# Sums of weight blocks made in DRAM by accumulating transfers, for twelve quads of a hybrid decoder trunk

## The chip, the cores and the metric

The kernel runs on one core of a Trainium2 chip. The metric is device time in microseconds of the whole program, the median of several runs. Engines are named as the profile names them: PE (TensorE), DVE (VectorE), ACT (ScalarE), POOL (GpSimd) and SP (SyncE). SP and POOL issue the DMA transfers here; the bytes are moved by 16 DMA engines that both queues share.

## The reference

Two layers on 512 tokens of width 1024, all float32. Layer 0 mixes with an mLSTM, layer 1 with a gated short convolution, and each is followed by a squared-ReLU MLP of width 4096:

```python
for i in range(DEPTH):
    h = rms_norm(x, g[0])
    h = mlstm_mixer(h, ...) if i % 2 == 0 else short_conv_mixer(h, ...)
    x = x + rms_norm(h, g[1])
    h = sqrelu_mlp(rms_norm(x, g[2]), w_mlp_up[i], w_mlp_down[i])
    x = x + rms_norm(h, g[3])
```

The products that matter here are `x @ w_up` (1024 x 4096, in both MLPs) and the convolution's input projection `x @ w_in` (1024 x 3072). In the mLSTM, each head's output is divided by its root mean square (`h * rsqrt(mean(h * h) + EPS)`) before the gate and the out projection.

## The kernel before

**Precision.** Every product is made of three fp32r products. A loaded weight block is split in a high half (ACT's cast, line 80) and a low half (DVE's subtraction, line 81), and `mm3` (lines 112 to 117) multiplies high by high, high by low and low by high.

**Quads.** The up projections and the convolution's input projection are computed by quads: a quad takes a 1024 x 512 piece of the weight as four blocks a, b, c, d of 512 x 256 (a and b the upper row half, c and d the lower) and forms the 2 x 2 block product with seven block products instead of eight. Four of the seven weight factors are sums of blocks: with the names of the new class `Sums` below f5 = a + b, f6 = f5 + d, f7 = b + d, f3 = f6 + c; the others are a, c and d themselves. Each block is loaded by SP into a "raw" tile of 512 KB (seven such buffers), DVE makes the sums in place (lines 899, 905, 920, 931 in `run`; lines 852 to 858 in `sums`, for a stage's first quad), and each factor is split as above.

**Stages.** There are three stages of quads: the MLP of layer 0 (eight quads), the convolution (six), and the MLP of layer 1 (eight). The first three quads of a stage (`AHEAD`) are prepared in `enter` while the stage before ends: their factors a and c are loaded and split, and their first two products run early. Later `run_first` and `run(True)` finish them.

**The mLSTM part**, in the first 187 us, holds no quads. It normalises x tile by tile (`pre_norm`; the power of the norm is a one-column operation of POOL, line 173), projects the first half of v, then the gates and q, k, then the second half of v with the chunk scores (`scores_and_core`), then the output gates, eight column pieces. `core` computes one chunk for two heads; its norm takes a power on POOL (line 714), between DVE's lines 713 and 715. The scaled result is transposed, gated and multiplied by the out projection.

**What sets the order.** The program is written as data flow; a scheduler places each engine's instructions by its own estimate of when they can start, and then each engine runs its list strictly in order. A transfer waits on its issuing engine, SP or POOL, until what it reads has landed and its buffer is free, and whatever stands behind it on that engine waits too. SP's transfers use eight semaphores in turn, and so do POOL's, so that at most eight of a queue are under way.

Of the kernel before, what the change touches and what calls it, by code (L numbers as in the profile page):

```python
# [8 lines left out]
F32 = mybir.dt.float32  # L9
# [3 lines left out]
ALU = mybir.AluOpType  # L13
# [26 lines left out]
def tile_hybrid_trunk(  # L40
# [239 lines left out]
    def last_product(wm, r0, hT, g, tail, accs=None, ends=False, ahead=None):  # L280

        flush()
        ws = {}
        parts = [halves() for _ in range(NT)]
        if ends:
            parts[NT - 1] = halves()[:1] + halves(4)[2:]
        ygs = [[] for _ in range(NT)]
        mss = [None] * NT

        def ks(o, t, cs, k0, k1):  # L290
            hf, c0 = divmod(cs.start, 512)
            n = cs.stop - cs.start
            for k in range(k0, k1):
                w = ws[hf][k // 2]
                mm3(
                    o[:, 0:n],
                    rows_of(hT, k, t),
                    (w[:, 0, k % 2, c0 : c0 + n], w[:, 1, k % 2, c0 : c0 + n]),
                    k == 0,
                    k == KO - 1,  # L300
                )

        def done(o, t, cs):
            n = cs.stop - cs.start
            step(BLOCK * n / 512)
            i = len(ygs[t])
            if i == 0:
                mss[t] = small(len(parts[t]))
            yg = half_kb(n=n) if accs is None else accs[t][:, cs]
            ygs[t].append((cs, yg))  # L310
            last = i == len(parts[t]) - 1
            o = o[:, 0:n]
            if accs is None:
                part_ms(o, mss[t], i)
                nc.vector.tensor_tensor(out=yg, in0=o, in1=g[:, cs], op=ALU.mult)  # L315
            else:
                y = accs[t][:, cs]
                nc.vector.tensor_tensor(out=y, in0=y, in1=o, op=ALU.add)  # L318
                part_ms(y, mss[t], i)
                eng = nc.vector if ends and t == NT - 1 else nc.gpsimd  # L320
                eng.tensor_tensor(out=yg, in0=y, in1=g[:, cs], op=ALU.mult)
            if last:
                tail(t, ygs[t], mss[t])

        for hf in range(2):
            ws[hf] = [
                piece(
                    wm[r0 + 2 * i * P : r0 + 2 * (i + 1) * P, halves()[hf]].rearrange(
                        "(k p) m -> p k m", p=P
                    ),  # L330
                    2,
                )
                for i in range(4)
            ]
            os = [pd() for _ in range(2)]
            first = KO - 2 if hf == 0 else 0
            for t in range(2):
                ks(os[t], t, parts[t][hf], 0, first)
            for t in range(2):
                ks(os[t], t, parts[t][hf], first, KO)  # L340
                done(os[t], t, parts[t][hf])
        for t in range(2, NT):
            if ahead is not None:
                ahead()
            for cs in parts[t]:
                o = pd()
                ks(o, t, cs, 0, KO)
                done(o, t, cs)


    wi = w_in_mlstm[0]
# [392 lines left out]
    def gated(j, sg):  # L744
# [7 lines left out]
        )  # L752
        put_pair(hT, j, pr)

    def scores_and_core(t):
        scores(t)
        if t > 0:
            core(t - 1, 0)

    v_half(1, [piece(v_src(1, i), 2) for i in range(4)], lambda t: None, scores_and_core)  # L760
    for j in range(KO):
        w = cols_piece(wi, 2 * QK + D + j * P)
        o = pu()
        proj_T(o, w, xT, 0, NT)
        take_o(j, o, BLOCK if j < KO - 1 else 0)
        if j <= NT:
            core((j - 1) % NT, 0 if j == 0 else 1)

# [37 lines left out]
    class Quad:  # L806

        def __init__(self, wm, c0, c1, xT, take, claim=lambda: None):  # L810
            self.wm, self.cols, self.xT, self.take = wm, (c0, c1), xT, take
            self.claim = claim

        def block(self, kh, nh):
            c = self.cols[nh]
# [30 lines left out]
            self.v = self.values()  # L846
            nc.scalar.copy(self.v, by_tile(self.x))

        def sums(self):
            tt = nc.vector.tensor_tensor  # L850
            a, b = self.block(0, 0), self.block(0, 1)
            tt(out=a, in0=a, in1=b, op=ALU.add)
            d = self.block(1, 1)
            t2 = raw_tile([4, 256])
            tt(out=t2, in0=a, in1=d, op=ALU.add)
            tt(out=b, in0=b, in1=d, op=ALU.add)
            c = self.block(1, 0)
            tt(out=c, in0=c, in1=t2, op=ALU.add)
            self.ts = c, a, t2, b, d

        def run_first(self):

            tt = nc.vector.tensor_tensor
            f = self.xT.f
            self.claim()
            o, z, y = pd(), pd(), self.y
            f4, f5, f6, f7, f3 = (self.factor(t) for t in self.ts)
            prod(o, f4, f["a22"], True)
            prod(z, f5, f["p1"], True)
            s5 = self.values()  # L870
            nc.scalar.copy(s5, by_tile(z))
# [12 lines left out]
            tt(out=s3, in0=by_tile(o), in1=s3, op=ALU.add)  # L884
            self.take(0, 1, s3, None)

        def run(self, begun):


            tt = nc.vector.tensor_tensor  # L890
            f = self.xT.f
            bank = pd if begun else pu
            self.claim()
            a, b = self.block(0, 0), self.block(0, 1)
            if not begun:
                self.f1 = self.factor(a)
                self.begin(pu)
            y = self.y
            tt(out=a, in0=a, in1=b, op=ALU.add)  # L899
            f5 = self.factor(a)  # L900
            z = bank()
            if not begun:
                prod(z, f5, f["p1"], True)
            d = self.block(1, 1)
            tt(out=a, in0=a, in1=d, op=ALU.add)  # L905
            f6 = self.factor(a)
            prod(y, f6, f["n2"], False)
            s5, s2 = self.values(), self.values()
            if begun:
                nc.scalar.copy(s2, by_tile(y))  # L910
                prod(z, f5, f["p1"], True)
            nc.scalar.copy(s5, by_tile(z))
            if not begun:
                nc.scalar.copy(s2, by_tile(y))
            c = self.block(1, 0)
            if not begun:
                self.f2 = self.factor(c)
                self.second()
                self.take(0, 0, self.values(), by_tile(self.x))
            tt(out=b, in0=b, in1=d, op=ALU.add)  # L920
            prod(y, self.factor(b), f["r3"], False)
            o = bank()
            nc.scalar.mul(by_tile(o), by_tile(y), -1.0)
            prod(z, self.factor(d), f["p4"], False)
            tt(out=s5, in0=by_tile(y), in1=s5, op=ALU.add)
            self.take(1, 1, s5, None)
            tt(out=s2, in0=by_tile(z), in1=s2, op=ALU.add)
            self.take(1, 0, s2, None)
            if begun:
                self.take(0, 0, self.v, None)  # L930
            tt(out=a, in0=a, in1=c, op=ALU.add)  # L931
            prod(o, self.factor(a), f["a22"], False)
            self.take(0, 1, self.values(), by_tile(o))

    def enter(quads):


        for qd in quads:
            qd.prepare()
        yield  # L940
        for qd in quads:
            qd.prepare_more()
        quads[0].sums()
        yield
        flush(2)
        for qd, bank in zip(quads, (pd, pd, pu)):
            qd.begin(bank)
        for qd in quads:
            qd.second()
            qd.put_by()  # L950
        flush()
# [4 lines left out]
    def mlp(i, xT, gain_of, tail_of, ends=False, ahead=None):  # L956
# [4 lines left out]
        def quad(g):  # L961
# [10 lines left out]
                    hs[j] = pair()  # L972
                split(hs[j][:, 0, half], hs[j][:, 1, half], c)

            return Quad(w_up[i], g * 512, g * 512 + 256, xT, take)

        ys = []

# [30 lines left out]
        quads[0].run_first()  # L1009
        quads[1].run(True)  # L1010
        for g in range(NG - 2):
            down(g)
            quads[g + 2].run(g + 2 < AHEAD)
            if g == NG - 4:
# [4 lines left out]
    def conv(xT, gain_of, tail_of, ahead):  # L1019
# [5 lines left out]
        def gated(p):  # L1025
# [33 lines left out]
                            op1=ALU.add,  # L1059
                        )  # L1060

            return Quad(wm, D + p * 256, 2 * D + p * 256, xT, take, claim)

        def out_gate(b):
            def take(nh, half, v, o):
# [4 lines left out]
                    yT[j] = pair()  # L1070
                split(yT[j][:, 0, half], yT[j][:, 1, half], v)

            return Quad(wm, b * 512, b * 512 + 256, xT, take)

        quads = [gated(0), gated(1), gated(2), out_gate(0), gated(3), out_gate(1)]
        first = quads[:AHEAD]
# [51 lines left out]
```

## Time and profile before

| | |
|---|---|
| median of 3 runs | 1106.7 us (1105.1 to 1108.88) |
| the profiled execution | 1111.46 us, its span 1109.7 us |
| granted TensorE clock, mean | 0.994 |
| moved by DMA | 133.73 MB, 121 GB/s over the span |
| read from HBM, written | 124.31 MB, 8.39 MB |

A span runs from the first to the last instruction. Times within the profile are microseconds from the span's start. In a timeline row the first two numbers are start and length, and the square bracket gives the engine's idle time before the instruction and what ended it. In a row of groups stand count, busy time, mean nanoseconds of one, and idle time ahead of it. Matmuls overlap, so that PE's busy time is not its work at full rate.

### The profile page before, as it was taken

The numbers are of one execution on the slowest core, as the hardware profiler recorded it, in microseconds if no ns is written. First come the engines' busy times: TensorE is split into PE (matmuls) and PEld (weight loads), VectorE is DVE, ScalarE is ACT, GpSimd is POOL, SyncE is SP. The second block draws the span as 40 slices with busy tenths as digits, with TensorE's granted clock in tenths as the row PEclk, the third lists the DMA queues.
The fourth block names the chain that finished last, engine by engine and source line by source line (L and its number), as shares of the span: only waits on it lengthen the run. The fifth ranks groups of instructions, "written<-read, shape, count | busy, mean of one in ns | idle before, by whom it ended". The sixth has DMA issues, their size and how long they took to land. (4 is left out here: it accounts for less than half of the span.)

```text
span 1109.7 us, 16027 instructions
## 1 busy us (share of the span) xinstructions
PE 1080.6 (97%) x6531; PEld 951.8 (86%) x6531; DVE 758.5 (68%) x1008; ACT 503.8 (45%) x780; POOL 70.3 (6%) x114
## 2 busy tenths in 40 slices
PE   7999999999999999999999999899999999999997
PEld 5878887789899899899879999778989989989986
DVE  5561567489776775758579998848967667575843
ACT  6441445365554244335346545636554434424521
POOL 1100010110000000000231000011000000000011
PEclk9999999999999999999999999989999999999999
DMA  8420264136344133163424362623533413415201
GB/s 266 134 76 1 76 228 138 71 102 198 117 135 134 46 126 125 47 208 110 144 89 153 95 209 96 200 105 104 182 117 128 135 56 114 133 44 203 96 19 57
DMA packets 104783, 133.73 MB, mean 121 GB/s; under 512 B 5221, under 2 KB 76165, under 8 KB 104710
## 3 DMA queue, kind: packets, MB, share of 16 engines
q1 hardware_dynamic: 100246, 116.46, 33.3%
q0 software_dynamic: 4464, 16.25, 4.0%
q8 instruction: 51, 0.84, 0.3%
q14 instruction: 22, 0.18, 0.1%
HBM read 124.31 MB, written 8.39 MB: 120 GB/s over the span
## 5 line engine op out<-in xcount | busy, mean ns | idle before, releaser
L81 DVE TENSOR_TENSOR u<-raw,u 128x1024 fp32r<-128x1024 f32 (+1 forms) x270 | 320.5, 1200 | 123.5 <-ACT u L80 123.1
L80 ACT CAST u<-raw 128x1024 fp32r<-128x1024 f32 (+1 forms) x270 | 272.3, 1028 | 216.2 <-PE pd L117 159.3
L115 PE MATMUL pu<-u 128*128 128x256 f32 (+1 forms) x1112 | 337.2, 303 | 3.5 <-ACT u L80 3.4
L116 PE MATMUL pu<-u 128*128 128x256 f32 (+1 forms) x1112 | 335.6, 302 | 0.8 <-DVE u L81 0.8
L117 PE MATMUL pu<-u 128*128 128x256 f32 (+1 forms) x1112 | 334.7, 301 | 0.8 <-DVE u L81 0.8
L115 PE MATMUL pd<-u,hb 128*128 128x512 f32 (+1 forms) x648 | 256.1, 395 | 5.5 <-DVE t L315 4.4
L116 PE MATMUL pd<-u,hb 128*128 128x512 f32 (+1 forms) x648 | 255.2, 394 | 0.0
L117 PE MATMUL pd<-u,hb 128*128 128x512 f32 (+1 forms) x648 | 255.1, 394 | 0.0
L115 PEld LDWEIGHTS pu<-u 128*128 128x128 f32 x1112 | 210.6, 189 | 13.7 <-ACT u L80 4.8
L116 PEld LDWEIGHTS pu<-u 128*128 128x128 f32 x1112 | 210.4, 189 | 10.1 <-DVE u L81 1.6
L117 PEld LDWEIGHTS pu<-u 128*128 128x128 f32 x1112 | 210.5, 189 | 9.6 <-DVE u L81 1.3
L115 PEld LDWEIGHTS pd<-u,hb 128*128 128x128 f32 x648 | 122.4, 189 | 35.2 <-DVE t L315 5.3
L117 PEld LDWEIGHTS pd<-u,hb 128*128 128x128 f32 x648 | 122.3, 189 | 28.2
L116 PEld LDWEIGHTS pd<-u,hb 128*128 128x128 f32 x648 | 122.5, 189 | 27.9 <-DVE u L81 0.6
L115 PE MATMUL pd<-u 128*128 128x256 f32 x312 | 88.3, 283 | 4.1 <-ACT pu L840 2.4
L116 PE MATMUL pd<-u 128*128 128x256 f32 x312 | 87.5, 281 | 0.0
L117 PE MATMUL pd<-u 128*128 128x256 f32 x312 | 87.3, 281 | 0.0
L1004 DVE TENSOR_TENSOR u<-u,pd 128x512 f32<-128x512 f32 x80 | 54.6, 683 | 36.8 <-PE pd L117 36.5
L181 ACT ACTIVATE junk<-u 128x512 bf16<-128x512 f32 (+1 forms) x49 | 30.5, 622 | 74.1 <-DVE u L318 53.3
L80 ACT CAST hb<-t 128x512 fp32r<-128x512 f32 x80 | 48.9, 619 | 32.5 <-DVE t L968 26.7
L115 PEld LDWEIGHTS pd<-u 128*128 128x128 f32 x312 | 58.8, 188 | 5.2 <-ACT pu L840 2.8
L116 PEld LDWEIGHTS pd<-u 128*128 128x128 f32 x312 | 58.8, 188 | 0.0
(173 smaller groups left out, 851.7 us busy)
## 6 DMA issues: line engine op xcount, KB each, us to landing
raw<-in_w_mlp_up_dram SPq DMA_DIRECT2D x76, 512.0 KB, 4.5
raw<-in_w_mlp_down_dram SPq DMA_DIRECT2D x64, 512.0 KB, 4.2
raw<-in_w_in_conv_dram SPq DMA_DIRECT2D x30, 512.0 KB, 4.8
raw<-in_w_in_mlstm_dram SPq DMA_DIRECT2D x24, 512.0 KB, 4.7
xd<-u POOLq DMA_DIRECT2D x12, 512.0 KB, 3.0
u<-xd POOLq DMA_DIRECT2D x12, 512.0 KB, 5.8
raw<-in_w_out_mlstm_dram SPq DMA_DIRECT2D x8, 512.0 KB, 4.1
raw<-in_w_out_conv_dram SPq DMA_DIRECT2D x8, 512.0 KB, 4.6
```

The costliest lines, as they stand in the source:

```text
L80: hi = nc.scalar.copy(dst_hi, src)
L81: lo = nc.vector.tensor_tensor(out=dst_lo, in0=src, in1=dst_hi.bitcast(F32), op=ALU.subtract)
L115: nc.tensor.matmul(o, lh, rh, start=first, stop=False, skip_group_check=True)
L116: nc.tensor.matmul(o, lh, rl, start=False, stop=False, skip_group_check=True)
L117: nc.tensor.matmul(o, ll, rh, start=False, stop=last, skip_group_check=True)
L181: nc.scalar.activation(junk(n), src, AF.Square, scale=float(D) ** -0.5, accum_out=ms[:, i : i + 1])
L1004: nc.vector.tensor_tensor(out=yh, in0=yh, in1=o, op=ALU.add)
```

## The change

For twelve quads (the three prepared ones of each MLP and all six of the convolution) the four sums are made in DRAM. `Sums` holds four DRAM tiles of 512 KB. Its stage 0 copies a, d, b and c into them on SP's queue, DRAM to DRAM; stages 1 to 3 add the rest by accumulating transfers on POOL's queue: b to f5 and d to f7, then f5 to f6, then f6 to f3. The quad then loads its four sums (`summed`), and a, c and d themselves where it needs them, seven loads in place of four blocks; the adds on DVE are gone for these quads. The sums of the first MLP are written in the loop of the second v half (stages 0 to 2) and of the output gates (stage 3); the nine others in the first MLP's `down` loop.

```diff
+    class Sums:
+        def __init__(self, wm, c0, c1):
+            def src(kh, c):
+                return wm[kh * 512 : (kh + 1) * 512, c : c + 256].rearrange("(p q) m -> q p m", q=P)
+            self.a, self.b, self.c, self.d = src(0, c0), src(0, c1), src(1, c0), src(1, c1)
+            self.f = [
+                dram.tile([P, 4, 256], F32, name=f"f{n}_{len(made)}") for n in (5, 6, 7, 3)
+            ]
+        def stage(self, i):
+            f5, f6, f7, f3 = self.f
+            if i == 0:
+                for f, blk in zip(self.f, (self.a, self.d, self.b, self.c)):
+                    nc.sync.dma_start(f, blk)
+                return
+            for f, blk in (((f5, self.b), (f7, self.d)), ((f6, f5),), ((f3, f6),))[i - 1]:
+                nc.gpsimd.dma_start(f, blk, accum_op=ALU.add, max_dma_last_dim=D)
...
     def scores_and_core(t):
+        if t != 2:
+            all_of(early, min(t, 2))
         scores(t)
...
         take_o(j, o, BLOCK if j < KO - 1 else 0)
+        if j == 3:
+            all_of(early, 3)
...
+        def summed(self, i):
+            raw = raw_tile([4, 256])
+            nc.sync.dma_start(raw, self.pre.f[i])
+            return self.factor(raw)
...
-            f4, f5, f6, f7, f3 = (self.factor(t) for t in self.ts)
+            f4, f5, f6, f7 = (self.summed(i) for i in (3, 0, 1, 2))
+            f3 = self.factor(self.block(1, 1))
...
-            tt(out=a, in0=a, in1=b, op=ALU.add)
-            f5 = self.factor(a)
+            if not pre:
+                tt(out=a, in0=a, in1=b, op=ALU.add)
+            f5 = self.summed(0) if pre else self.factor(a)
...
-        quads[0].sums()
...
         for g in range(NG - 2):
+            if i == 0:
+                for k in range(3):
+                    if 0 <= g - k < 4:
+                        all_of(later[3 * k : 3 * k + 3], g - k)
             down(g)
```

The new lines shift the rest: the norm's power on POOL is line 743 after the change (714 before), DVE's step behind it line 744 (715), the copies are line 367 and the accumulating transfers line 370.

On SP's queue before the change, in the mLSTM part: the q and k pieces and the second v half's four pieces (shape 128x2x512) are followed at once by the eight output-gate pieces (128x8x128) and the out projection.

```order
L98 DMA raw<-in_w_in_mlstm_dram 128x8x128 x8
L98 DMA raw<-in_w_in_mlstm_dram 128x2x512 x2
L724 DMA t_702<-in_w_conv_dram 24x128
L725 DMA t_702<-in_g_hnorm_dram 8x128
L98 DMA raw<-in_w_in_mlstm_dram 128x2x512 x2
L98 DMA raw<-in_w_in_mlstm_dram 128x8x128 x8
L98 DMA raw<-in_w_out_mlstm_dram 128x2x512 x3
```

After the change, the same place; `f_3` to `f_11` are the sums of the convolution's quads and of the second MLP's, four tiles to a number. Shown are the last of the four v pieces with what follows it, and then the end of that run of copies.

```order
L98 DMA raw<-in_w_in_mlstm_dram 128x2x512
L367 DMA f_2_720<-in_w_mlp_up_dram 512x1x256
L367 DMA f_3_721<-in_w_in_conv_dram 512x1x256
L367 DMA f_3_722<-in_w_in_conv_dram 512x1x256
L367 DMA f_3_723<-in_w_in_conv_dram 512x1x256
```

```order
L367 DMA f_11_753<-in_w_mlp_up_dram 512x1x256
L367 DMA f_11_754<-in_w_mlp_up_dram 512x1x256
L98 DMA raw<-in_w_in_mlstm_dram 128x8x128 x3
L367 DMA f_11_755<-in_w_mlp_up_dram 512x1x256
L367 DMA f_11_756<-in_w_mlp_up_dram 512x1x256
L98 DMA raw<-in_w_in_mlstm_dram 128x8x128 x5
```

Between the last v piece and the first three output-gate pieces now stand 35 copies, those of the convolution and of the second MLP among them; all 48 copies are ahead of the fourth output-gate piece.

On POOL before the change, in the same part: the memsets of the gate rows, the four selections of the decay matrix (line 610), the eight powers of the head norm (line 714), and then the first out-projection norm.

```order
L522 MEMSET u 4x512
L589 MEMSET sel 36x512
L523 MEMSET u 4x4
L610 AFFINE_SELECT hb<-hb 128x512 x4
L714 TENSOR_TENSOR small<-small,mhalf 128x2 x8
L173 TENSOR_TENSOR small<-small,mhalf 128x1
```

After the change, around the first two of the eight powers (now line 743):

```order
L370 DMA f_7_740<-f_7_738 512x256
L370 DMA f_9_747<-in_w_mlp_up_dram 512x1x256
L370 DMA f_8_744<-f_8_742 512x256
L743 TENSOR_TENSOR small<-small,mhalf 128x2
L370 DMA f_10_749<-in_w_mlp_up_dram 512x1x256
L370 DMA f_9_746<-f_9_745 512x256
L370 DMA f_10_751<-in_w_mlp_up_dram 512x1x256
L370 DMA f_10_750<-f_10_749 512x256
L370 DMA f_11_753<-in_w_mlp_up_dram 512x1x256
L370 DMA f_9_748<-f_9_746 512x256
L370 DMA f_10_752<-f_10_750 512x256
L743 TENSOR_TENSOR small<-small,mhalf 128x2
```

Of the 48 accumulating transfers, four stand among the four powers of the first norm, 34 between these and the first head-norm power, seven between the first and the second, three between the second and the third; the other powers follow without any between them. The list of DVE in this part reads as before.

More of the change, by code (lines that the diff above doesn't have):

```diff
@@ L348, in last_product, with sums_of @@
                 done(o, t, cs)
+    class Sums:
[14 more added lines that the diff above has]
+                nc.gpsimd.dma_start(f, blk, accum_op=ALU.add, max_dma_last_dim=D)
+    made = {}
+    def sums_of(key, wm, cols):
+        for c in cols:
+            made[key, c[0]] = Sums(wm, *c)
+        return [made[key, c[0]] for c in cols]
     wi = w_in_mlstm[0]
@@ L753, in gated, with up_cols, all_of @@
         put_pair(hT, j, pr)
+    def up_cols(gs):
+        return [(g * 512, g * 512 + 256) for g in gs]
+    early = sums_of(0, w_up[0], up_cols(range(AHEAD)))
+    later = sums_of(
+        "conv",
+        w_in_conv[0],
+        [(D + p * 256, 2 * D + p * 256) for p in range(3)]
+        + up_cols([0])
+        + [(D + 768, 2 * D + 768)]
+        + up_cols([1]),
+    ) + sums_of(1, w_up[1], up_cols(range(AHEAD)))
+    def all_of(sums, i):
+        for sm in sums:
+            sm.stage(i)
     def scores_and_core(t):
+        if t != 2:
+            all_of(early, min(t, 2))
         scores(t)
@@ L806, in tile_hybrid_trunk, with __init__ @@
     class Quad:
-        def __init__(self, wm, c0, c1, xT, take, claim=lambda: None):
+        def __init__(self, wm, c0, c1, xT, take, key, claim=lambda: None):
             self.wm, self.cols, self.xT, self.take = wm, (c0, c1), xT, take
             self.claim = claim
+            self.pre = made.get((key, c0))
         def block(self, kh, nh):
@@ L847, in put_by @@
             nc.scalar.copy(self.v, by_tile(self.x))
[L849 to L859, printed above, removed]
+        def summed(self, i):
+            raw = raw_tile([4, 256])
+            nc.sync.dma_start(raw, self.pre.f[i])
+            return self.factor(raw)
         def run_first(self):
@@ L892, in run @@
             bank = pd if begun else pu
+            pre = self.pre is not None
             self.claim()
-            a, b = self.block(0, 0), self.block(0, 1)
+            if not pre:
+                a, b = self.block(0, 0), self.block(0, 1)
             if not begun:
-                self.f1 = self.factor(a)
+                self.f1 = self.factor(self.block(0, 0) if pre else a)
                 self.begin(pu)
             y = self.y
-            tt(out=a, in0=a, in1=b, op=ALU.add)
-            f5 = self.factor(a)
+            if not pre:
+                tt(out=a, in0=a, in1=b, op=ALU.add)
+            f5 = self.summed(0) if pre else self.factor(a)
             z = bank()
@@ L903, in run @@
                 prod(z, f5, f["p1"], True)
-            d = self.block(1, 1)
-            tt(out=a, in0=a, in1=d, op=ALU.add)
-            f6 = self.factor(a)
+            if not pre:
+                d = self.block(1, 1)
+                tt(out=a, in0=a, in1=d, op=ALU.add)
+            f6 = self.summed(1) if pre else self.factor(a)
             prod(y, f6, f["n2"], False)
@@ L914, in run @@
                 nc.scalar.copy(s2, by_tile(y))
-            c = self.block(1, 0)
+            if not pre or not begun:
+                c = self.block(1, 0)
             if not begun:
@@ L919, in run @@
                 self.take(0, 0, self.values(), by_tile(self.x))
-            tt(out=b, in0=b, in1=d, op=ALU.add)
-            prod(y, self.factor(b), f["r3"], False)
+            if not pre:
+                tt(out=b, in0=b, in1=d, op=ALU.add)
+            prod(y, self.summed(2) if pre else self.factor(b), f["r3"], False)
             o = bank()
             nc.scalar.mul(by_tile(o), by_tile(y), -1.0)
-            prod(z, self.factor(d), f["p4"], False)
+            prod(z, self.factor(self.block(1, 1) if pre else d), f["p4"], False)
             tt(out=s5, in0=by_tile(y), in1=s5, op=ALU.add)
@@ L930, in run @@
                 self.take(0, 0, self.v, None)
-            tt(out=a, in0=a, in1=c, op=ALU.add)
-            prod(o, self.factor(a), f["a22"], False)
+            if not pre:
+                tt(out=a, in0=a, in1=c, op=ALU.add)
+            prod(o, self.summed(3) if pre else self.factor(a), f["a22"], False)
             self.take(0, 1, self.values(), by_tile(o))
@@ L973, in take @@
                 split(hs[j][:, 0, half], hs[j][:, 1, half], c)
-            return Quad(w_up[i], g * 512, g * 512 + 256, xT, take)
+            return Quad(w_up[i], g * 512, g * 512 + 256, xT, take, i)
         ys = []
@@ L1060, in take @@
                         )
-            return Quad(wm, D + p * 256, 2 * D + p * 256, xT, take, claim)
+            return Quad(wm, D + p * 256, 2 * D + p * 256, xT, take, "conv", claim)
         def out_gate(b):
@@ L1071, in take @@
                 split(yT[j][:, 0, half], yT[j][:, 1, half], v)
-            return Quad(wm, b * 512, b * 512 + 256, xT, take)
+            return Quad(wm, b * 512, b * 512 + 256, xT, take, "conv")
         quads = [gated(0), gated(1), gated(2), out_gate(0), gated(3), out_gate(1)]
```

## The prediction

> **What bounds the kernel now.** I read the page's first part, then the busy time by stages, then the timelines of GpSimd, VectorE and SyncE in the first 140 us, because the change puts nearly all its new transfers there.
>
> ```profile
> span 1109.7 us, 16027 instructions
> PE 1080.6 (97%) x6531; PEld 951.8 (86%) x6531; DVE 758.5 (68%) x1008; ACT 503.8 (45%) x780; POOL 70.3 (6%) x114
> ```
>
> TensorE is busy all but 29.1 us of the span, so a lighter VectorE can give back little, and only where TensorE waits for it. By stages (columns: stretch, its length, busy us of PE, PEld, DVE, ACT, POOL, granted clock, DMA share, GB/s):
>
> ```profile
> 0.00:28.00 28.00, 22.04 (x77) 14.37 (x78) 15.50 (x28) 17.48 (x34) 4.96 (x19) 1.00 0.88 263
> 8.00:14.00 6.00, 4.78 (x13) 3.10 (x12) 3.63 (x4) 4.56 (x8) 0.00 (x0) 1.00 1.03 395
> 28.00:56.00 28.00, 28.00 (x126) 22.78 (x125) 14.52 (x22) 13.33 (x17) 3.33 (x7) 1.00 0.46 133
> 56.00:84.00 28.00, 26.52 (x114) 20.39 (x113) 17.20 (x26) 10.81 (x26) 2.49 (x4) 1.00 0.28 76
> 84.00:112.00 28.00, 28.00 (x134) 22.74 (x133) 5.79 (x17) 3.44 (x9) 0.79 (x2) 1.00 0.00 1
> 224.00:308.00 84.00, 82.04 (x554) 74.54 (x553) 70.53 (x89) 49.50 (x79) 5.38 (x8) 1.00 0.45 144
> 560.00:588.00 28.00, 26.64 (x155) 22.87 (x154) 23.77 (x34) 16.71 (x34) 10.81 (x12) 1.00 0.26 87
> 588.00:672.00 84.00, 79.67 (x670) 78.88 (x668) 78.30 (x93) 48.03 (x67) 4.25 (x12) 1.00 0.47 153
> 672.00:728.00 56.00, 51.78 (x348) 48.09 (x347) 43.30 (x47) 28.62 (x38) 0.00 (x0) 0.91 0.53 170
> 756.00:812.00 56.00, 54.54 (x430) 52.54 (x428) 52.24 (x70) 31.35 (x50) 3.00 (x5) 1.00 0.49 156
> ```
>
> The last five rows hold the twelve quads: VectorE is 77 to 93% busy there and TensorE idles 2.0 + 1.4 + 4.3 + 4.2 + 1.5 = 13.4 us. That, and 5 us of lost clock in 672 to 728 (0.09 x 56), is all that fewer adds could return. The first rows are the mLSTM part, where the DMA is nearly idle from 56 to 112 us and TensorE full.
>
> In that part TensorE hangs on a short VectorE-GpSimd chain, the power of the head norm (line 714, on GpSimd). Timelines of GpSimd and VectorE:
>
> ```profile
> 110.38 0.72 POOL L714 TENSOR_TENSOR small<-small,mhalf 128x2 f32<-128x2 f32 x1 [26.32 <-DVE small L713]
> 120.68 0.70 POOL L714 TENSOR_TENSOR small<-small,mhalf 128x2 f32<-128x2 f32 x1 [9.58 <-DVE small L713]
> 132.83 0.69 POOL L714 TENSOR_TENSOR small<-small,mhalf 128x2 f32<-128x2 f32 x1 [11.44 <-DVE small L713]
> ```
> ```profile
> 111.14 0.16 DVE L715 TENSOR_TENSOR small<-small 128x2 f32<-128x2 f32 x1 [0.84 <-POOL small L714]
> 111.34 0.62 DVE L718 TENSOR_SCALAR u<-u,small 128x256 f32<-128x256 f32 x2
> 115.36 0.69 DVE L641 TENSOR_TENSOR raw<-pd,hb 128x512 f32<-128x512 f32 x1 [3.40 <-PE pd L638]
> ```
>
> VectorE takes its instructions in order: line 715 waits for the first power, and behind it stands line 641, which empties a PSUM bank that TensorE fills again at once. VectorE idles 3.40 us before line 641, so the first power may come up to 3.4 us late, at 113.8 us, before TensorE stops.
>
> **The change part by part.** *Adds removed.* Each of twelve quads loses four adds on 128x1024, as in these groups and in lines 852 to 858:
>
> ```profile
> L899 DVE TENSOR_TENSOR raw<-raw 128x1024 f32<-128x1024 f32 x19 | 23.1, 1217 | 0.3 <-DMA raw<-in_w_in_conv_dram 0.2
> L852 DVE TENSOR_TENSOR raw<-raw 128x1024 f32<-128x1024 f32 x3 | 3.7, 1217 | 0.0
> ```
>
> 48 x 1.217 = 58 us of VectorE work go. Of the 13.4 us and 5 us above I credit 7 us net, because TensorE's waits there also end at ScalarE's copies and at PSUM, and because new idle stretches will cost clock. The range of this term is 0 to 18.
>
> *Loads.* Nine quads load seven blocks where they loaded six, three load seven where they loaded four: 18 more transfers of 512 KB in stages where the DMA share is at most 0.53. Hidden; their buffers come free after one split instead of several adds.
>
> *Copies and accumulates.* 48 copies on SyncE's queue and 48 accumulating transfers on GpSimd's, 512 KB each. The order shows where they stand: all of them in the mLSTM part, those for the convolution and the second MLP too, since nothing in them depends on the stage in which they are written. On SyncE's queue 35 copies stand between the last value-weight load (issued at 55.17 us) and the first three output-gate loads. On GpSimd's, 34 accumulates stand between the last power of the first norm (line 173) and the first head-norm power, 7 more ahead of the second, 3 more ahead of the third. An accumulate waits for its copy and, two or three rows on, for the accumulate before it; the powers queue behind. That GpSimd holds everything behind a waiting transfer is seen already in the view of waits, where its loads of x wait for TensorE:
>
> ```profile
> POOL u L776 <- PE pu L117: 470.3, 5, 229.9
> ```
>
> The load on SyncE's queue behind which the copies now stand (timeline of SyncE), the queue's totals (packets, MB, share of 16 engines) and GpSimd's issue of a 128-row transfer (groups):
>
> ```profile
> 55.17 0.39 SPq L98 DMA_DIRECT2D raw<-in_w_in_mlstm_dram  x1
> ```
> ```profile
> q1 hardware_dynamic: 100246, 116.46, 33.3%
> ```
> ```profile
> L785 POOL DMA_DIRECT2D xd<-u x12 | 7.0, 584 | 24.1 <-DVE u L274 24.1
> ```
>
> The price of a transfer: SyncE's queue moved 116.46 MB in 33.3% of 1109.7 us, 315 GB/s while busy, so 1.66 us for 512 KB (0.524 MB). The fastest stretch, 8 to 14 us with the queue never empty, moved 395 GB/s: 1.33 us. With the queue kept full I take 1.5 for a copy. No row shows an accumulate. Below: one pass, like a copy, at 1.33. Above: three passes (source, destination, write) at 1.66, 5.0 us. I take two passes, 3.0 us, as both addends must be read.
>
> DMA work ahead of the first power, counted from 28 us: the loads of before, 0.46 x 28 + 0.28 x 28 = 20.7, less three output-gate loads that now queue behind (5.0), 15.7; what the first 28 us (12% of them free, 3.4 us) can't hold of the first quad's four copies and four accumulates, 6 + 12 - 3.4 = 14.6; 35 copies, up to the one that the last of these accumulates needs, 52.5; 34 accumulates, 102. Sum 185 us: the first power at 213 instead of 110.4, 99 us past 113.8. The second power: seven accumulates, each sharing with a copy or load, 7 x 4.5 = 31.5 against 10.3 before, +21. The third: 3 x 4.5 plus latency against 12.2, +4. Then GpSimd is free and the rest runs as before. GpSimd's own issuing (0.58 us for a transfer of 128 rows; these have 512, so up to 2.3) stays below 4.5 and is hidden.
>
> *The start.* Four copies (6 us) go ahead of the last two x loads, and four accumulates between GpSimd's powers of the first norm. Most of it falls on tiles whose turn on TensorE comes later, so I take 2 us; the bounds are 0 and 8.
>
> Sum: 99 + 21 + 4 + 2 - 7 = +119 us. The profiled execution took 1111.46 us for a span of 1109.7, 4.8 above the median of 1106.7; the terms are differences, so I add them to the median: 1226 us.
>
> The Trainium skill ("DMA: Bandwidth & Descriptors", Anatomy of one DMA) fits a GpSimd transfer as 2.0 us plus bytes over 436 GB/s, 1.2 us of streaming for 512 KB, an estimate that counts one pass; by 1.2 for copies and accumulates alike the sum would be about +21, 1128 us. This trace's best stretch (395 GB/s) stays below that rate, and no run here shows it for DRAM to DRAM.
>
> **The rivals.** *One pass* (0.2): an accumulate costs what a copy costs. Work ahead of the first power at 1.33: 15.7 + 7.2 + 46.6 + 45.2 = 115, power at 143, 29 late; second +8; with +2 and -7 that is +32, 1139 us. At 1.66 it is 1169. For it: 395 GB/s were reached. Against: two operands must come in. The Trainium skill's fit ("DMA: Bandwidth & Descriptors", Anatomy of one DMA) counts bytes once and so describes this rival.
>
> *Three passes or worse* (0.18): accumulates of 5.0 us, or descriptors that GpSimd writes as slowly. Copies at 1.66: 15.7 + 23.1 + 58.1 + 169 = 266, power at 294, 180 late; second +36, third +8; 1326 us. Nothing in the trace speaks for or against.
>
> *Hidden, and faster* (0.05): the idle DMA takes the sums for nothing and the twelve quads get their 58 us of VectorE back. The price is the -7 (0 to -18): 1100 us. It decides at 113.8 us: the 69 transfers would have to land in 86 us less the 15.7 of other loads, 1.0 us each or 515 GB/s, above any stretch of the trace. It needs the accumulates not to gate the power.
>
> *No effect* (0.02): sums hidden and TensorE's waits in the quads not VectorE's adds at all, 1107.
>
> **How the numbers follow.** Two passes has 0.55 (1200 to 1250 with copies from 1.33 to 1.66). Leaving out the outer tails of the two neighbours, the range is 1140 to 1325. All three DMA cases are slower: 0.93. This kernel's runs resolve about 0.3%, 3.3 us; within that 0.02, faster 0.05.
>
> **What would show it.** DMA share near 1 from about 30 us to past 200 us where it was 0.00 to 0.46. The first power (now line 743) near 213 us, released by a DMA or by GpSimd's own queue; VectorE's line 744 idle for about 100 us ahead of it, and TensorE with it. From the second half of the out projection on, the stages as long as before, the quads' a little shorter. Wrong, if the first power is issued before 120 us, if TensorE's loss lies after 300 us, or if the accumulates land in under 2 us each with the queue full.

## The result, and the profile after

The changed kernel takes 1224.1 us (median, 1221.7 to 1224.8) where the kernel before takes 1107.8: ratio 1.105, 95% interval 1.101 to 1.108. It is slower by 116 us; +119 was forecast. The profiled execution took 1224.8 us, with a span of 1223.1.

From the page of the changed kernel's profile: engines, granted clock and DMA share in 40 slices of 30.6 us, and the two queues (packets, MB, share of 16 engines).

```profile
PE 1090.4 (89%) x6531; PEld 959.8 (78%) x6531; DVE 708.9 (58%) x960; ACT 504.1 (41%) x780; POOL 121.7 (10%) x162
...
PEclk9899655689999999999999999999999999999999
DMA  9999999976227244223416256773373333135111
...
q1 hardware_dynamic: 116662, 151.07, 39.0%
q0 software_dynamic: 29808, 41.42, 16.5%
```

VectorE's 48 adds are gone and its busy time is 50 us lower, as meant. The DMA digits read 9 through the first eight slices, 245 us, where the page of before has a 2 in the third and a 0 in the fourth. POOL's queue went from 4.0 to 16.5% of the engines' time. The loss is early, as the busy time by stages shows (columns as in the prediction):

```profile
28.00:56.00 28.00, 22.06 (x86) 17.94 (x87) 9.24 (x15) 7.90 (x14) 6.18 (x13) 0.82 1.10 279
...
84.00:112.00 28.00, 28.00 (x124) 21.69 (x123) 2.60 (x5) 6.14 (x19) 5.87 (x6) 1.00 1.16 265
112.00:140.00 28.00, 5.82 (x27) 4.41 (x25) 0.72 (x2) 0.59 (x1) 9.09 (x10) 0.68 1.17 248
...
168.00:196.00 28.00, 0.00 (x0) 0.00 (x0) 0.00 (x0) 0.00 (x0) 8.93 (x8) 0.50 1.18 238
```

TensorE does nothing from 168 to 196 us while the DMA share is 1.18. What it hangs on are POOL's selections of the decay matrix (line 639) and powers of the head norm (line 743), shown first in POOL's timeline, then in VectorE's, then as seen by TensorE in the view of waits:

```profile
137.06 2.19 POOL L639 TENSOR_SCALAR_AFFINE_SELECT hb<-hb 128x512 f32<-128x512 f32 x2
...
203.87 1.03 POOL L370 DMA_DIRECT2D f<-f  x1 [8.73 <-DMA f<-f]
204.52 1.13 POOL L743 TENSOR_TENSOR small<-small,mhalf 128x2 f32<-128x2 f32 x1
236.27 1.13 POOL L743 TENSOR_TENSOR small<-small,mhalf 128x2 f32<-128x2 f32 x1
252.01 1.11 POOL L743 TENSOR_TENSOR small<-small,mhalf 128x2 f32<-128x2 f32 x1
...
299.82 0.69 POOL L743 TENSOR_TENSOR small<-small,mhalf 128x2 f32<-128x2 f32 x1 [9.55 <-DVE small L742]
```
```profile
139.28 0.69 DVE L670 TENSOR_TENSOR raw<-pd,hb 128x512 f32<-128x512 f32 x1 [33.48 <-POOL hb L639]
...
205.69 0.16 DVE L744 TENSOR_TENSOR small<-small 128x2 f32<-128x2 f32 x1 [58.16 <-POOL small L743]
```
```profile
PE pd L702 <- DVE raw L670: 54.1, 1, 54.1
PE pd L667 <- DVE raw L670: 22.2, 1, 22.2
PE pd L709 <- DVE raw L670: 20.0, 1, 20.0
```

Each of the three waits ends at VectorE's line 670, which empties a bank of scores. The 22.2 us come first: line 670 waits there for the selections. In the other two it stands behind line 744, which waits for a power; the first power runs right behind an accumulate (line 370) that had to wait for another one. On SyncE's queue (timeline) the copies go out one in 3.5 us, later one in 4.4, and the first three output-gate loads behind them only at 197.72:

```profile
69.45 84.45 SPq L367 DMA_DIRECT2D f<-in_w_in_conv_dram  x24
153.94 43.68 SPq L367 DMA_DIRECT2D f<-in_w_mlp_up_dram  x10
197.72 21.03 SPq L98 DMA_DIRECT2D raw<-in_w_in_mlstm_dram  x3
```

The eighth power is 126.1 us later than before (299.82 for 173.72), but the span only 113.4 longer: 12.7 us came back later. They came back in one place. Stores of x at the end of the first MLP and of the convolution, of the kernel before and of the changed one:

```profile
553.29 0.63 POOL L785 DMA_DIRECT2D xd<-u  x1 [1.74 <-DVE u L274]
...
734.46 0.58 POOL L785 DMA_DIRECT2D xd<-u  x1 [1.75 <-DVE u L274]
```
```profile
678.34 0.62 POOL L835 DMA_DIRECT2D xd<-u  x1 [1.75 <-DVE u L274]
...
847.09 0.58 POOL L835 DMA_DIRECT2D xd<-u  x1 [1.75 <-DVE u L274]
```

The convolution took 181.17 us from store to store and takes 168.75, 12.4 less. After that, up to the end, it was 375.2 and is 376.0. The convolution's quads, 126 us later than before, are now without gaps and at full clock (1.56 us idle, where the same stretches had 8.6 and a clock of 0.91):

```profile
714.00:798.00 84.00, 82.54 (x697) 82.15 (x698) 64.29 (x75) 48.69 (x66) 3.06 (x9) 1.00 0.68 225
798.00:854.00 56.00, 55.90 (x357) 50.21 (x356) 38.55 (x49) 28.95 (x45) 2.91 (x6) 1.00 0.53 172
```

### The profile page after: what moved, and what is told of

Its sections match the earlier page's. It is cut to its first block, busy times and chain, and to the rows that moved or that the text cites. A ratio compares the mean times of both kernels' runs of the same rounds, so it can differ in the third digit from the quotient of the medians.

```text
span 1223.1 us, 16189 instructions
## 1 busy us (share of the span) xinstructions
PE 1090.4 (89%) x6531; PEld 959.8 (78%) x6531; DVE 708.9 (58%) x960; ACT 504.1 (41%) x780; POOL 121.7 (10%) x162
## 3 DMA queue, kind: packets, MB, share of 16 engines
q0 software_dynamic: 29808, 41.42, 16.5%
## 5 line engine op out<-in xcount | busy, mean ns | idle before, releaser
L181 ACT ACTIVATE junk<-u 128x512 bf16<-128x512 f32 (+1 forms) x49 | 30.6, 624 | 80.1 <-DVE u L318 56.9
```

The source lines that it names most:

```text
L181: nc.scalar.activation(junk(n), src, AF.Square, scale=float(D) ** -0.5, accum_out=ms[:, i : i + 1])
```

## Experiments

The theory to be tested: an accumulate takes more engine time than a copy, a pair about 4.4 us. Pairs fill the 16 engines from the start to 250 us, and two queues that run in order carry that to TensorE: POOL's (selections and powers behind accumulates) and SyncE's (output-gate loads behind 35 copies). The rivals: the copies alone do it; GpSimd's writing of descriptors or the waits from one accumulate to the next do it; POOL's queue alone does it; or the DMA work costs its time wherever it stands.

| run | time, us | ratio to before, 95% |
|---|---|---|
| copies only | 1097.5 | 0.990 to 0.993 |
| plain transfers for accumulates | 1163.3 | 1.048 to 1.053 |
| nine quads' accumulates behind the out projection | 1128.6 | 1.017 to 1.021 |
| nine quads' copies and accumulates in the first MLP | 1182.1 | 1.066 to 1.070 |
| no sums, only the loads | 1096.9 | 0.989 to 0.992 |
| five rows of transfers by themselves | 1267.0 | single run |
| no early sums, accumulates unpaced | 1109.4 | 1.000 to 1.002 |
| no early sums, accumulates paced | 1097.5 | 0.989 to 0.992 |
| selections and powers on VectorE | 1218.2 | 1.098 to 1.102 |
| early sums only, behind the first norm's powers | 1119.0 | 1.008 to 1.012 |
| early sums only, as they stood | 1120.5 | 1.009 to 1.013 |
| sums for the convolution alone, paced | 1097.5 | 0.989 to 0.992 |

**Copies only.**

```diff
-                nc.gpsimd.dma_start(f, blk, accum_op=ALU.add, max_dma_last_dim=D)
+                pass
```

> The 48 copies stay, the 48 accumulating transfers are left out (the quads then load plain blocks in place of sums, so the products are of other numbers). Theory of two passes (a copy 1.5 us of the 16 engines, an accumulate about 2.9, 4.4 a pair): from 28 us the o-gate loads have 15.7 us of loads and 41 copies, 62 us, ahead of them, 78 in all of the 84 up to 112 us; nearly hidden, first head-norm power at 110 to 122, time 1095 to 1115, with 10 to 13 us given back in the quads. Rival, the copies are the cost (4.4 us each, because they go DRAM to DRAM in 1 KB rows): 15.7 + 41 x 4.4 = 196, first power near 220, time about 1200.

Measured: 1097.5 us, first head-norm power at 109.65. SyncE's timeline has the same two runs of copies as above:

```profile
55.46 37.00 SPq L367 DMA_DIRECT2D f<-in_w_in_conv_dram  x24
92.50 17.19 SPq L367 DMA_DIRECT2D f<-in_w_mlp_up_dram  x10
109.78 7.47 SPq L98 DMA_DIRECT2D raw<-in_w_in_mlstm_dram  x3
```

34 copies leave in 54.2 us, 1.6 us each, and the output-gate loads are issued at 109.78, in time. All 48 copies are hidden. The rival that they are the cost falls.

**Plain transfers in place of accumulates.**

```diff
-                nc.gpsimd.dma_start(f, blk, accum_op=ALU.add, max_dma_last_dim=D)
+                nc.gpsimd.dma_start(f, blk, max_dma_last_dim=D)
```

> Each accumulating transfer becomes a plain transfer of the same shape on the same queue with the same waits (it overwrites where it added, so the products are of other numbers). Theory of two passes: a transfer of one pass costs 1.5 like a copy, the pair 3.0 instead of 4.4; first power near 156, time 1139 to 1169. Rival, the pair takes 4.4 us because GpSimd writes 512 rows of descriptors or because each transfer waits for the one it builds on: nothing changes, first power near 204, time about 1224.

Measured: 1163.3 us, first power at 164.93. Same number of transfers, same order, same waits, and half of the loss is gone. So about half of it is what adding costs more than copying; the rest comes with 48 more transfers on full engines. Descriptors and waits alone would have left 1224.

**The price by itself.** To the kernel before, behind its last store:

```diff
+    for n in range(N):
+        nc.gpsimd.dma_start(f[n], f[n - 6], accum_op=ALU.add, max_dma_last_dim=D)
+    for n in range(N):
+        nc.gpsimd.dma_start(f[n], blk(n + N + 8), accum_op=ALU.add, max_dma_last_dim=D)
+    for n in range(N):
+        nc.gpsimd.dma_start(f[n], blk(n), max_dma_last_dim=D)
```

with 12 copies and 12 accumulates ahead, and 12 plain transfers from sums behind; N is 12.

> The kernel before, and behind its last store five rows of twelve transfers of 512 KB each, with nothing beside them: 12 copies on SyncE's queue; on GpSimd's 12 accumulates from weight blocks (1 KB rows), 12 from other sums (4 KB rows), 12 more from weight blocks, 12 plain transfers from weight blocks, 12 plain ones from sums. Theory of two passes: in the rows of accumulates alone one lands every 2.7 to 3.3 us, in the plain rows one every 1.4 to 1.7; time about 1107 + 12 x 1.5 + 36 x 3 + 24 x 1.55 = 1270. Rival, one pass: both land every 1.4 to 1.7, time about 1215. Rival, 1 KB rows are what costs: the second row of accumulates (4 KB) lands twice as fast as the third. Rival, GpSimd's writing of descriptors: the plain rows are as slow as the accumulates.

Measured: 1267.0 us. Stretches of 15 us in the second row of accumulates (4 KB rows), the third (1 KB rows), the first plain row (1 KB) and the second (4 KB); the last number is GB/s:

```profile
1170.00:1185.00 15.00, 0.00 (x0) 0.00 (x0) 0.00 (x0) 0.00 (x0) 6.25 (x6) 0.50 1.24 197
...
1200.00:1215.00 15.00, 0.00 (x0) 0.00 (x0) 0.00 (x0) 0.00 (x0) 4.73 (x6) 0.50 1.24 198
...
1230.00:1245.00 15.00, 0.00 (x0) 0.00 (x0) 0.00 (x0) 0.00 (x0) 4.54 (x7) 0.50 1.01 320
1245.00:1260.00 15.00, 0.00 (x0) 0.00 (x0) 0.00 (x0) 0.00 (x0) 4.38 (x7) 0.50 1.02 318
```

0.524 MB at 197 GB/s are 2.66 us for an accumulate; at 318 GB/s a plain transfer takes 1.65. The two add up to 4.3, the changed kernel's pair to 4.4. The length of the rows makes no difference that counts, and one pass, 1.65 for both, is out.

**The nine later quads' accumulates behind the out projection's last store**, on POOL's queue, the copies unmoved:

```diff
+                        with tc.issue_after(stores[-1].ins):
+                            all_of(later[3 * k : 3 * k + 3], g - k)
```

> The 36 accumulates of the convolution and the second MLP are put behind the last store of the out projection on GpSimd's queue; their 36 copies stay where they were, so does all of the first three quads. Theory of two causes side by side (GpSimd's queue holds the powers, and the o-gate loads stand behind the copies on SyncE's queue): 12 pairs x 4.4 less 3.4, 49, and 15.7 of loads and 34 copies, 51, make 116 us from 28, so the o-gate loads land near 144 and TensorE loses 20 to 40 us; time 1110 to 1140. Rival, GpSimd's queue alone: the powers come at 122 (12 late from the start) and the time is 1095 to 1112. Rival, bytes alone, wherever the accumulates stand: 36 x 2.9 = 104 us are only moved to a later stage and the time stays above 1180.

Measured: 1128.6 us. The powers are on time but for the start. TensorE stops once, for 11.1 us, at an output-gate load (SyncE's timeline, then ScalarE's, whose split of that load TensorE waits for):

```profile
121.48 16.93 SPq L367 DMA_DIRECT2D f<-in_w_mlp_up_dram  x10
138.51 9.25 SPq L98 DMA_DIRECT2D raw<-in_w_in_mlstm_dram  x3
```
```profile
149.44 1.04 ACT L80 CAST u<-raw 128x1024 fp32r<-128x1024 f32 x1 [11.38 <-DMA raw<-in_w_in_mlstm_dram]
```

The 36 accumulates now fill the engines from 280 to 420 us, at a DMA share of 1.13 to 1.20. TensorE is busy for 24.51 of the first 28 us of this, at a clock of 0.94, and throughout from 308 us on: most of their engine time is hidden, so the work does not cost its time wherever it stands. The run moves the engine time and the queue together, though, so it cannot say which of the two queues held the kernel.

**Selections and powers on VectorE**, all transfers unmoved:

```diff
-        nc.gpsimd.affine_select(out=DT[:, h, :, :], in_=DT[:, h, :, :], ...)
+        nc.vector.tensor_tensor(
+            out=DT[:, h, :, :], in0=DT[:, h, :, :],
+            in1=keep.unsqueeze(1).broadcast_to([P, NT, P]), op=ALU.min)
...
-        nc.gpsimd.tensor_tensor(out=f, in0=f, in1=mhalf, op=ALU.pow)
+        nc.vector.reciprocal(f, f)
```

> The changed kernel, every transfer where it was, but the decay selections and the head-norm powers are done on VectorE (a minimum with a mask, and a reciprocal in place of the power, so the head norm scales by other numbers); no accumulate stands ahead of them any more. Theory of two gates: the copies still land one in 4.4 us because each shares the engines with an accumulate, and the first three o-gate loads stand behind 35 of them, so TensorE still stops, near 205 us instead of 207; the blocks and the out projection then run without further stops, where they met three more powers before: out projection from about 270 instead of 313, time 1160 to 1215. Rival, GpSimd's queue alone: 1108 to 1130, as in the run that put the accumulates behind the out projection's store.

Measured: 1218.2 us, 6 less than with all of it on POOL, and 3 above the expected range. No power waits for an accumulate, and yet TensorE stops for 71.2 us in one wait (waits, SyncE's timeline, ScalarE's):

```profile
PE pu L115 <- ACT u L80: 76.6, 2, 71.2
```
```profile
69.20 84.97 SPq L378 DMA_DIRECT2D f<-in_w_in_conv_dram  x24
154.21 35.75 SPq L378 DMA_DIRECT2D f<-in_w_mlp_up_dram  x10
190.06 16.05 SPq L98 DMA_DIRECT2D raw<-in_w_in_mlstm_dram  x3
```
```profile
210.34 1.04 ACT L80 CAST u<-raw 128x1024 fp32r<-128x1024 f32 x1 [71.49 <-DMA raw<-in_w_in_mlstm_dram]
```

The copies leave nearly as slowly as in the changed kernel, since each shares the engines with an accumulate, and the output-gate loads behind them are issued at 190 us, where they were at 198. POOL's queue alone is not the cause: behind it stands a second wait, almost as long. The reverse was not run: that the selections and powers behind the accumulates would hold TensorE as long with the output-gate loads in time is read from the waits of the changed kernel, not tested. The Trainium skill ("DMA: Bandwidth & Descriptors", Issuing engines are not separate DMA queues) says that transfers run on the same 16 engines whichever engine starts them; here that agrees: a copy on SyncE's queue takes 1.6 us alone and, in the changed kernel, 3.5 to 4.4 beside accumulates on POOL's.

**The same work in the first MLP, where the code has it.** Copies and accumulates of the nine quads:

```diff
+                        with tc.issue_after(stores[-1].ins), tc.issue_after(loads[-1].ins):
+                            all_of(later[3 * k : 3 * k + 3], g - k)
```

> Copies and accumulates of the convolution and the second MLP are held in the first MLP, where the code has them: behind the load that precedes them on SyncE's queue, behind the out projection's last store on GpSimd's. The first three quads' stay as they are. Theory: 15.7 + 49 of the 84 us before 112, so only the start is late (about 12 us); the first MLP has 0.55 x 336 = 185 us of free DMA time for 36 x 4.4 = 158; the quads give back 10 to 13. Time 1100 to 1125, the upper part if 12 copies in a row ahead of the down weights let TensorE wait. Rival, the pair costs no engine time of its own but blocks queues: 1095 to 1100. Rival, bytes alone: above 1180.

Measured: 1182.1 us, a miss by 57. The mLSTM part is short again but for the start. The loss lies between 280 and 476 us, and there the copies have found other loads to stand ahead of (SyncE's and ScalarE's timelines, and TensorE's longest wait):

```profile
311.54 38.77 SPq L367 DMA_DIRECT2D f<-in_w_in_conv_dram  x12
350.41 7.92 SPq L98 DMA_DIRECT2D raw<-in_w_mlp_down_dram  x4
```
```profile
367.14 1.04 ACT L80 CAST u<-raw 128x1024 fp32r<-128x1024 f32 x1 [28.31 <-DMA raw<-in_w_mlp_down_dram]
368.09 0.58 ACT L963 COPY t<-pd 128x512 f32<-128x512 f32 x1
```
```profile
PE pd L115 <- ACT t L963: 24.8, 1, 24.8
```

Twelve copies in a row at 3.2 us hold back the down weights. ScalarE waits 28 us for one of them, a PSUM copy (line 963) stands behind that, and TensorE waits for the copy's bank. My sum of free engine time (185 us for 158) was no argument: a stage with room on the engines has none on a queue whose next load is due.

**What the adds are worth.**

```diff
-                nc.sync.dma_start(f, blk)
-                nc.gpsimd.dma_start(f, blk, accum_op=ALU.add, max_dma_last_dim=D)
...
-            nc.sync.dma_start(raw, self.pre.f[i])
+            nc.sync.dma_start(raw, (self.pre.a, self.pre.d, self.pre.b, self.pre.c)[i])
```

> No copies and no accumulates; the quads load seven blocks and add nothing (plain blocks stand in for the sums, so the products are of other numbers). What the 48 adds are worth, with their extra loads and nothing else. Theory: with all copies still in, the time was 1097.5, and those were hidden; so 1094 to 1099, 9 to 13 us under the kernel before. Rival, the 18 more loads take back part of the gain: the same 1094 to 1099 with the copies, too, would then not separate them, but 1085 to 1090 here would show that copies cost 8 to 12 us.

Measured: 1096.9 us, 11 below the kernel before, and 0.6 us below the run with all copies: this is what leaving out the 48 adds gives, with the 18 additional loads.

**Without early sums**: the first MLP's quads add on VectorE as before, the copies of the other nine stay in the mLSTM part, and their accumulates stand in the first MLP. First all at its start:

```diff
-    early = sums_of(0, w_up[0], up_cols(range(AHEAD)))
+    early = []
...
+                        with tc.issue_after(stores[-1].ins):
+                            all_of(later[3 * k : 3 * k + 3], g - k)
```

> The first MLP's three quads add on VectorE as before; the other nine keep their sums, their copies stay in the mLSTM part, their accumulates stand behind the out projection's last store on GpSimd's queue. Theory: no accumulate stands ahead of a power, so the start and the mLSTM part cost nothing; the convolution and the second MLP give back 8 us (those stages gained that in the run without accumulates); the first MLP, with 36 accumulates of 2.9 us against its own loads, loses 0 to 6. Time 1099 to 1106. Rival, accumulates anywhere cost their DMA time: 36 x 2.9 = 104, above 1150.

Measured: 1109.4 us, no gain, and 3 above the expected range. The convolution's 12 us are back, and the first MLP's quads lose as much (busy time by stages; before, TensorE was busy for 28.00 and 27.39 us of these stretches at clock 1.00):

```profile
252.00:280.00 28.00, 24.10 (x188) 23.48 (x187) 20.82 (x28) 11.23 (x17) 9.43 (x9) 0.94 1.16 262
280.00:308.00 28.00, 24.10 (x130) 20.47 (x129) 16.45 (x21) 12.43 (x18) 6.27 (x6) 0.88 1.18 235
```

The loads of these quads land late (VectorE's timeline, TensorE's wait):

```profile
291.68 1.22 DVE L964 TENSOR_TENSOR raw<-raw 128x1024 f32<-128x1024 f32 x1 [3.93 <-DMA raw<-in_w_mlp_up_dram]
```
```profile
PE pd L115 <- DVE t L1038: 3.9, 1, 3.9
```

VectorE waits 3.93 us to add a block that has not landed, line 1038 stands behind that add, and TensorE waits for line 1038. No copy stands ahead of these loads on SyncE's queue. From 252 to 308 us they take 10.9 us from issue to landing (median), where the kernel before takes 4.8: engines filled by accumulates are enough to make a load late.

Then paced, by an element of the previous group's down product that POOL must wait for:

```diff
+                if g > 0:
+                    gate = nc.gpsimd.tensor_copy(small(), ys[NT - 1][:, D - 1 : D])
...
+                        with tc.issue_after(gate.ins):
+                            all_of(later[3 * k : 3 * k + 3], g - k)
```

> As the run before it in this list, but the accumulates are spread over the first MLP: before those of each group of features GpSimd copies one element that the previous group's down product wrote, and so waits for it. Theory: DMA share there stays under about 1 and TensorE finds its loads in time; 1097 to 1101, 7 to 10 us under the kernel before. Rival, full DMA engines do no harm as long as no load stands behind a copy on SyncE's queue: the same time as unpaced.

Measured: 1097.5 us, ratio 0.991 (0.989 to 0.992): 0.9% faster than the kernel before. But not for the reason given: the DMA share was not kept under 1, and yet TensorE never waits in these stretches.

```profile
392.00:420.00 28.00, 28.00 (x171) 24.87 (x170) 22.41 (x27) 11.67 (x15) 7.71 (x7) 1.00 1.18 234
420.00:448.00 28.00, 28.00 (x205) 26.43 (x204) 17.70 (x21) 13.61 (x18) 7.32 (x7) 1.00 1.19 235
```

In these 56 us the loads of up weights take 8.9 us to land (median), and there is time for that. What the gate does is to hold the first accumulate until 306 us, where unpaced it was issued at 243, in the midst of the loads for the stage's first quads. Later the same full engines do no harm. The gate both starts the accumulates later and spreads them; no run separates the two.

**The start**, tried with sums for the first MLP's three quads alone (the list `later` is empty, and the other nine add as before), once with the accumulates behind the first norm's fourth power and once as they stood:

```diff
         if t != 2:
-            all_of(early, min(t, 2))
+            with tc.issue_after(norms[NT - 1].ins):
+                all_of(early, min(t, 2))
```

> Only the first MLP's three quads keep their sums (12 copies, 12 accumulates), and the accumulates are put behind the fourth power of the first norm; the other nine quads add on VectorE as before. Theory, that the start lost its 12 us because accumulates stood ahead of the first norm's powers on GpSimd's queue: TensorE busy over 27 of the 28 us from 28, time 1104 to 1111. Rival, full DMA engines delay the x loads: 22 to 24 us busy, time 1114 to 1121.

> As the run before it in this list, but the accumulates stand where the changed kernel has them, four of them among the powers of the first norm. Theory: 12 us slower than that run, 1116 to 1123, with two powers of the first norm 6 and 12 us late. Rival: no difference between the two.

Measured: 1119.0 and 1120.5 us, no difference that counts, where 12 us were expected. The second run's powers are late as in the changed kernel. In the first they are on time and TensorE is busy from 28 to 66 us, and then it stops: the accumulates now stand ahead of POOL's memsets for the gates (POOL's timeline; VectorE's; TensorE's wait).

```profile
49.46 1.01 POOL L372 DMA_DIRECT2D f<-f  x1 [13.95 <-DMA f<-in_w_mlp_up_dram]
...
53.76 0.19 POOL L554 MEMSET u<- 4x4 f32 x1
```
```profile
53.97 1.16 DVE L623 CAST sel<-ident 4x128 fp32r<-4x128 f32 x3 [7.86 <-POOL u L554]
```
```profile
PE pt L598 <- DVE t L586: 9.6, 1, 9.6
```

VectorE's casts (line 623) wait for the last memset, what stands behind them on VectorE comes some 7 us late, and at 66 us TensorE waits for it. The theory of the start was right on the queue and wrong on the row: behind the powers is the next instruction that someone waits for. Full engines delaying the x loads are not needed to explain it.

**The convolution alone.** Of the paced run, only its 24 copies and 24 accumulates:

```diff
-    ) + sums_of(1, w_up[1], up_cols(range(AHEAD)))
+    )
...
-                for k in range(3):
+                for k in range(2):
```

> As the paced run, but only the convolution's six quads take sums (24 copies, 24 accumulates); the six quads of the two MLPs add on VectorE as in the kernel before. Theory, that the whole gain lies between the first MLP's last product and the convolution's, where the changed kernel took 168.75 us for 181.17 and its MLPs no less than before: 1095 to 1099, no slower than with nine or twelve quads. Rival, each quad's adds are worth the same: half of the gain, 1101 to 1104.

Measured: 1097.5 us, ratio 0.990 (0.989 to 0.992). Six quads give what nine give, and what leaving out the adds of all twelve gives.

## Why the prediction was right

**The place and the gates.** Forecast: 35 copies and 34 accumulates ahead of the first head-norm power, which comes at 213 us; it came at 204.5. That the powers gate TensorE is shown by the waits. Two gates were not named. The selections on POOL stopped TensorE first, 22.2 us at 117.8 us, within the time that the power took anyway. And the output-gate loads behind the copies would have kept nearly all of the loss (1218 us) without the powers. I counted these copies as work ahead of the power, and so the sum held although it named one gate of two. VectorE's line 744 was idle for 58 us ahead of the first power and not for about 100, because the selections had held VectorE before that.

**The prices.** Copies: 1.5 taken, 1.6 measured. Accumulates: 3.0 taken, 2.66 measured. With the measured prices the same sum is 15.7 + 13.6 + 35 x 1.6 + 34 x 2.66 = 176, the power at 204; it was seen at 204.5. The two errors had opposite signs; together they made the forecast of the power 8.5 us too late. An accumulate takes 1.6 times a plain transfer, not twice, so its price lies between one pass and two: that it costs more than a copy is shown, that it makes two passes is not. Issuing one took POOL 1.03 to 1.23 us, less than the 2.3 allowed for.

**Second and third power.** +21 and +4 forecast; the gaps of 31.75 and 15.74 us for 10.30 and 12.15 make +21.4 and +3.6. Not forecast were 6.9 us more between the third and the eighth power (47.81 for 40.89), where TensorE again meets late loads.

**The start.** 2 us forecast (0 to 8): mis-sized. It lost about 11: in 28 to 56 us 5.9 of idle time and 0.18 of the clock, 5. I looked at both copies ahead of x loads and accumulates between POOL's powers. The copies cost nothing (copies only: first power at 109.65). The accumulates ahead of POOL's small operations cost all of it. In the sum this loss vanished, since the power at 204.5 was set by the transfers and not by when TensorE began.

**The quads.** -7 credited, -12.7 measured: mis-sized, within its bounds. I took less than the 13.4 idle us and 5 us of clock because the waits also end at ScalarE and PSUM. In the kernel before, 7.6 of the 9.8 us that TensorE waits from 560 to 728 us, the convolution's quads, end at VectorE, and nearly all of the idle time and all of the lost clock there went. In the quads of each MLP the longest of its waits, 1.2 us, ends at ScalarE (line 840), and the 24 adds there were worth nothing (-1.1 us between the stores of the first, +0.8 from the convolution's store to the end), although VectorE was 93% busy in those of the second MLP.

**The sum.** 94.1 + 21.4 + 3.6 + 6.9 - 12.7 = +113.3 for the span's +113.4, and +116 by the medians. In the forecast's terms the first power is 5 us less, the start 2 and the quads 6, and 7 us were not forecast at all. That these errors leave the sum within 3 us of the median is luck; the place, the gate that was named and most of the size are not.

**The rivals.** One pass was priced at 1139 to 1169, and the run that has one pass took 1163. Hidden and faster was priced at 1100 with 1.0 us a transfer; kernels that hide the sums of nine or of six quads take 1097.5. What the rival needed was not faster transfers but accumulates some 200 us later, and none for the first MLP. Three passes were priced at 5.0 us an accumulate; 2.66 rules them out. The Trainium skill's fit for a GpSimd transfer ("DMA: Bandwidth & Descriptors", Anatomy of one DMA), 1.2 us of streaming for 512 KB by an estimate from it, is below both measured prices, 1.65 and 2.66.

## What to carry to other kernels

Work without dependences goes where the scheduler thinks it free, not where the code has it; on a queue that runs in order it then stands ahead of what is due. Ask of each moved transfer which instruction stands behind it on its queue, and after that which one is next: taking one gate away (powers, 6 us) or going past one row (the start, 1.5 us) gave next to nothing, because another gate lay right behind. And put the relief only where TensorE waits for the relieved engine, which that engine's busy share does not tell: the convolution's six quads were worth all of the gain, and half of the transfers bought it.

## What the runs showed of the hardware

- An accumulating transfer of 512 KB, DRAM to DRAM, takes 2.66 us of the 16 engines, a plain one 1.65, whether its rows are 1 or 4 KB long. That is 1.6 times, not twice. The page of the profile counts the bytes of an accumulate once: HBM reads rose by 59.8 MB, which 48 copies, 48 accumulates and 18 loads of 0.524 MB make without a second operand (114 x 0.524 = 59.8). That both addends are read, as I argued for two passes, is thus not shown by bytes; shown is that the transfer costs more. The Trainium skill ("DMA: Bandwidth & Descriptors", Rules for kernel authors) states that an accumulate reads its destination and writes it later; where that read goes in the counters stays open.
- The DMA share reads 1.13 to 1.24 where accumulates fill the engines and 1.01 to 1.05 where plain transfers do; in these runs a share above 1 goes with transfers that stand in line.
- Beside accumulates that fill the engines, a load of up weights takes 8.9 to 10.9 us from issue to landing, where it took 4.8. That does not always stop TensorE: in the paced run it is busy for 56 us on end at a share of 1.18. Nor does a stop need copies ahead of the loads on SyncE's queue: in the unpaced run, without any there, TensorE was idle for 7.8 of 56 us at 1.16 to 1.18. With copies ahead (the nine quads' copies and accumulates in the first MLP) it stopped for longer, 24.8 us in one wait at 1.14 to 1.16.
